# Neighbourhood attention scores: two heads on the two halves of the partitions, three 64-row products each

## The chip, the core and the metric

One NeuronCore of a Trainium2 chip runs the whole program: two layers of a transformer-like trunk on 512 latent and 256 context tokens of 1024 features. The metric is the device time of one execution in microseconds (us), lower is better. The engines are TensorE (PE, its weight loads PEld), VectorE (DVE), ScalarE (ACT), GpSimd (POOL) and SyncE (SP, which issues most DMAs). Each engine works through its own queue in order; a semaphore makes it wait for another one.

## The reference, cut to what matters

The neighbourhood attention has 4 heads of 64 features. A latent token attends to 8 x 32 = 256 latent tokens around it, with a bias that also masks, and to the 256 context tokens; a context token attends to the context only.

```python
q, k, v = jnp.split(p, 3, axis=-1)
q, k = _rms(_heads(q, NA_HEADS), g_q), _rms(_heads(k, NA_HEADS), g_k)
...
s_loc = jnp.einsum('bhrjqd,bhrjkd->bhrjqk', qg, kb).astype(F32) * scale + bias[None]
s_ctx = jnp.einsum('bhrjqd,bhcd->bhrjqc', qg, kc).astype(F32) * scale
p = jax.nn.softmax(jnp.concatenate([s_loc, s_ctx], axis=-1), axis=-1).astype(v.dtype)
o = (jnp.einsum('bhrjqk,bhrjkd->bhrjqd', p[..., :n_loc], vb)
     + jnp.einsum('bhrjqc,bhcd->bhrjqd', p[..., n_loc:], vc))
```

The kernel computes the products of two float32 operands as three products of their high and low parts (high x high, high x low, low x high), which TensorE takes in its faster 32-bit type (fp32r).

## The kernel before

Features lie on the partitions for most products, 128 at a time. A layer is: modulated norm; input projections (for MLA, Hyena and the neighbourhood heads); the neighbourhood attention woven with a Hyena convolution; MLA's attention; output projection; MLP.

*Making queries and keys* (`na_qk`): for keys, then queries, the projection gives 128 tokens on the partitions and 256 features (4 heads) at a time. The tokens are squared, summed and, for keys, scaled by their 1 / rms. A group of two or three token tiles is then transposed by TensorE (L513), two heads (`hp`) at a time, so that head 2 hp has partitions 0 to 63 and head 2 hp + 1 partitions 64 to 127 of a PSUM tile `t`. The split takes each head for itself. For a query, ScalarE copies the high part to the head's own half of `na.q` (L518), and VectorE subtracts it and writes the low part to the *other* half (L519): a column of `na.q[:, h]` holds high and low parts one under the other, 128 rows. For a key, ScalarE copies the high part to its own half of `na.k` (L523), VectorE writes the low part to `na.kl` (L524), and ScalarE copies the high part once more, to the other half of `na.k` (L525).

*Scores* (`na_scores`, for one head, 128 queries and 256 keys) are two matmuls into the same PSUM columns: one on all 128 rows (L550), which gives high x high and low x high together, and one on the 64 rows of the high part with `na.kl` (L552).

*Attention* (`na_attend`) works in units of 128 queries and two heads: 8 units for latent queries in each layer, and 4 for context queries in the first layer alone. A unit's `scores` fill a PSUM tile `s_` of two banks, one for each head, 256 local and 256 context keys: eight matmuls for a latent unit, four for a context unit. VectorE adds the bias (L575), ScalarE copies the context part (L576), then come the softmax (`softmax_rows`, L447 to L460), the transposes of the weights two units later (`turn`, L587), and the product with the values two units after that (`output`, L606: the two heads on two halves of the array's columns). There are two PSUM tiles of `s_`'s kind at this time.

The program is written as generators that take turns (`weave`), here attention with the Hyena convolution at 1 : 1.4; a scheduler then sets the order on each engine from what depends on what. Tiles are placed in SBUF by pools on a left and a right stack; a tile that comes to lie where another one was waits for that one's users.

Of the kernel before, what the change touches and what calls it, by code (L numbers as in the profile page):

```python
# [16 lines left out]
ALU = mybir.AluOpType  # L17
# [19 lines left out]
def r32(ap):  # L37
    return ap.bitcast(F32)
# [3 lines left out]
def kernel(ctx, tc, A, dbg=None, stop=None):  # L42
# [22 lines left out]
    def psum_banks(mm):  # L65
        """all of PSUM: mm tiles of two banks, the rest tiles of one"""
# [52 lines left out]
    def rsqrt(p, out, ms):  # L119
        """out = ms ** -0.5 for ms > 0"""  # L120
# [7 lines left out]
    def mm3(out, s, m, start, stop):  # L128
        """out += (sh + sl).T @ (mh + ml) but for sl.T @ ml"""
# [44 lines left out]
    def modulation_rows(lv, cr, p):  # L174
        """the same by dot products off the tensor engine, features on the partitions"""
# [34 lines left out]
    def sumsq(acc, xT, k, nt, p):  # L210
        """acc += xT[:, k] ** 2"""
# [7 lines left out]
    def norm_rstd(acc, nt, p):  # L219
        """the tokens' 1 / rms, on every partition; comes last, after a turn for others"""  # L220
# [24 lines left out]
    def norm_h(l, n, xT, hh, hl, nt, p):  # L245
        """modulated activations of normed ones, a tile of features at a time"""
# [10 lines left out]
    def norm_stream(l, s, rb, xT, hh, hl, p):  # L257
        """norm_x and norm_h of a stream"""
# [25 lines left out]
    def gemm(out, w, nk, m, streams, woff=0, wstride=128, fill=iter(())):  # L284
        """out[:, tokens] = W.T @ act: w's and m's high and low parts; outs, ws and streams may be lists, k's then shared"""
# [42 lines left out]
    def sin_layer(p, outs, zs, hyc, j):  # L328
        """sin(freq (z + b)) by way of the remainder of the argument by 2 pi; a layer on each half"""
# [15 lines left out]
    def filter_hidden(p, h2):  # L345
        """the filters' hidden activations, both layers', and a row of ones"""
# [15 lines left out]
    def filter_unit(l, st, o, h2, fc, dec, w3, p):  # L362
        """a filter of a layer, stream and order: generators for the time domain and for the spectrum"""
# [60 lines left out]
    def na_bias(l, p, sc):  # L424
        """relative position biases, [query, column block kind, head, key], NEG_INF outside the window"""
# [17 lines left out]
    def softmax_rows(p, sb, n, nh, tag, scale=None, src=None):  # L443
        """sb[:, h, :n] = softmax of scale * src[:, h, :n] over n, for the heads h"""
# [20 lines left out]
    def token_gemm(pts, grp, n, hh, hl, w, fill=iter(())):  # L465
        """pts[token tile][:, :n] = act[:, token tile].T @ w for the token tiles of the group"""
# [13 lines left out]
    def na_v(l, hh, hl, na, kr, fill=iter(())):  # L480
        """values of the neighbourhood heads and MLA's shared rope key, tokens on the partitions"""
# [72 lines left out]
    def na_attend(l, na, nb, mh, ml, p):  # L554
# [5 lines left out]
        def scores(u):  # L560
# [3 lines left out]
            if j >= 4:  # L564
                for hh in range(2):
                    na_scores(s_[:, hh, 0:256], na, 2 * hp + hh, 128 * j, S, 256)
# [1002 lines left out]
```

## Time and profile before

| | |
|---|---|
| runs | 1871.37, 1879.92, 1880.49 us |
| median | 1879.92 us |
| span of the profiled execution, first to last instruction | 1876.5 us |
| TensorE matmul / weight load busy | 96% / 81% |
| VectorE / ScalarE / GpSimd busy | 66% / 44% / 18% |
| mean granted TensorE clock | 0.975 |

For the profiled execution the span is the time that is known; it lies 3.4 us under the median of the runs. Busy shares are means over stages with different limits. "Busy" on TensorE is from a matmul's start to its modelled end, and these overlap, so that 96% doesn't say that it multiplies all the time: the distance from one start to the next does. In the timeline a row is a run of like instructions with its start, its length, the engine, the line and the tiles (out<-in), and in square brackets the idle time of the engine before it and what ended it.

### The profile page before, as it was taken

The numbers are of one execution on the slowest core, as the hardware profiler recorded it, in microseconds if no ns is written. First come the engines' busy times: TensorE is split into PE (matmuls) and PEld (weight loads), VectorE is DVE, ScalarE is ACT, GpSimd is POOL, SyncE is SP. The second block draws the span as 40 slices with busy tenths as digits, with TensorE's granted clock in tenths as the row PEclk, the third lists the DMA queues.
The fourth block names the chain that finished last, engine by engine and source line by source line (L and its number), as shares of the span: only waits on it lengthen the run. The fifth ranks groups of instructions, "written<-read, shape, count | busy, mean of one in ns | idle before, by whom it ended". The sixth has DMA issues, their size and how long they took to land.

```text
span 1876.5 us, 27190 instructions
## 1 busy us (share of the span) xinstructions
PE 1797.2 (96%) x10722; PEld 1519.0 (81%) x10722; DVE 1232.1 (66%) x2127; ACT 824.1 (44%) x1387; POOL 338.1 (18%) x265
## 2 busy tenths in 40 slices
PE   6999978999998999999999999899999999999999
PEld 2688877766686878888888888788777799999997
DVE  5866775866668865666665447887877665555554
ACT  3334435566644543333334124555566653333331
POOL 1523320300034423323232000530300000000000
PEclk9999987999999899999999999899999999999999
DMA  8124423052143333333333212254040022322322
GB/s 336 59 84 144 149 94 100 23 212 62 54 179 124 135 122 123 124 135 127 121 117 120 68 63 94 86 198 138 25 176 24 23 91 90 98 94 90 101 91 79
DMA packets 73247, 205.08 MB, mean 109 GB/s; under 512 B 12540, under 2 KB 24589, under 8 KB 71840
## 3 DMA queue, kind: packets, MB, share of 16 engines
q1 hardware_dynamic: 71520, 198.10, 30.9%
q0 software_dynamic: 1600, 5.24, 0.7%
q8 instruction: 85, 1.39, 0.3%
q14 instruction: 42, 0.34, 0.1%
HBM read 181.30 MB, written 21.23 MB: 108 GB/s over the span
## 4 chain that ended last, share of the span: by engine, by line
PE 66%; DVE 7%; issue 2%; ACT 2%; DMA 2%; POOL 1%; SPq 0%; DVEq 0%; POOLq 0%; ACTq 0%
PE mm L295 46%; PE b L1040 3%; PE mm L1027 3%; PE mm L1374 2%; PE mm L131 2%; PE mm L132 2%; PE mm L133 2%; PE b L1081 1%; DMA wm<-in_w_modr_dram 1%; DVE wm L193 1%; DVE wl L137 1%; PE mm L987 1%; POOL wmp L189 1%; PE b L150 1%; DVE t L1380 1%
## 5 line engine op out<-in xcount | busy, mean ns | idle before, releaser
L295 PE MATMUL mm<-t,wh 128*128 128x512 f32 (+1 forms) x2496 | 495.0, 319 | 1.9 <-DVE t L1064 1.3
L295 PEld LDWEIGHTS mm<-t,wh 128*128 128x128 f32 x2496 | 373.3, 190 | 38.0 <-issue 2.4
L136 ACT ACTIVATE wh<-wr 128x1024 fp32r<-128x1024 f32 (+2 forms) x176 | 184.6, 1050 | 419.1 <-PE mm L295 399.7
L295 PE MATMUL mm<-t,wl 128*128 128x512 f32 (+1 forms) x1248 | 298.5, 317 | 0.0
L189 POOL TENSOR_TENSOR wmp<-wm,t 128x1024 f32<-128x1024 f32 x64 | 169.5, 2655 | 487.1 <-DMA wm<-in_w_modr_dram 314.2
L137 DVE TENSOR_TENSOR wl<-wr,wh 128x1024 fp32r<-128x1024 f32 (+2 forms) x176 | 224.0, 1273 | 35.3 <-ACT wh L136 31.9
L295 PE MATMUL mm<-ah,wh 128*128 128x512 f32 (+1 forms) x768 | 232.8, 357 | 3.9 <-DVE t L1064 3.2
L295 PE MATMUL mm<-al,wh 128*128 128x512 f32 (+1 forms) x768 | 231.9, 356 | 0.0
L295 PE MATMUL mm<-ah,wl 128*128 128x512 f32 (+1 forms) x768 | 231.3, 356 | 0.0
L1064 DVE SCALAR_TENSOR_TENSOR t<-mm,mods,t 128x512 f32<-128x512 f32 x216 | 135.9, 657 | 134.3 <-PE mm L295 127.6
L295 PEld LDWEIGHTS mm<-t,wl 128*128 128x128 f32 x1248 | 194.7, 190 | 16.9
L193 DVE SCALAR_TENSOR_TENSOR wm<-wm,t 128x1024 f32<-128x1024 f32 x64 | 91.1, 1426 | 104.6 <-POOL wmp L189 104.6
L295 PEld LDWEIGHTS mm<-ah,wh 128*128 128x128 f32 x768 | 127.0, 189 | 27.4 <-DVE t L1064 3.5
L295 PEld LDWEIGHTS mm<-al,wh 128*128 128x128 f32 x768 | 127.6, 189 | 20.6
L295 PEld LDWEIGHTS mm<-ah,wl 128*128 128x128 f32 x768 | 126.6, 189 | 21.6
L194 ACT ACTIVATE wmp<-wmp 128x1024 f32<-128x1024 f32 x64 | 67.9, 1060 | 147.3 <-POOL wmp L189 147.3
L137 DVE TENSOR_TENSOR al<-relu,ah 128x768 fp32r<-128x768 f32 (+1 forms) x64 | 68.0, 1064 | 37.2 <-ACT ah L136 37.1
L447 DVE TENSOR_REDUCE mmx<-mm 128x1 f32<-128x768 f32 (+1 forms) x80 | 67.7, 847 | 32.1 <-PE mm L133 31.5
L452 ACT ACTIVATE msb<-mm,mmx,qrs 128x768 f32<-128x768 f32 (+1 forms) x80 | 72.2, 903 | 23.3 <-DVE mmx L449 19.4
L1374 PE MATMUL mm<-t,wh 128*128 128x512 f32 x320 | 76.8, 354 | 2.8 <-DVE t L1064 2.8
L1028 ACT ACTIVATE mpt<-mm 128x768 f32<-128x768 f32 (+1 forms) x80 | 57.6, 725 | 49.4 <-PE mm L1027 49.3
L136 ACT ACTIVATE ah<-relu 128x768 fp32r<-128x768 f32 (+1 forms) x64 | 47.3, 739 | 63.9 <-DVE relu L1127 63.7
(316 smaller groups left out, 3070.2 us busy)
## 6 DMA issues: line engine op xcount, KB each, us to landing
wr<-in_w_ff_dram SPq DMA_DIRECT2D x128, 512.0 KB, 3.6
wm<-in_w_modr_dram SPq DMA_DIRECT2D x64, 512.0 KB, 4.5
wm<-in_w_mod_dram SPq DMA_DIRECT2D x32, 512.0 KB, 7.7
wr<-in_w_in_t_dram SPq DMA_DIRECT2D x18, 512.0 KB, 3.3
qk<-qk_spill SPq DMA_DIRECT2D x9, 576.0 KB, 5.9
qk_spill<-upk SPq DMA_DIRECT2D x12, 384.0 KB, 3.0
kx<-kk POOLq DMA_DIRECT2D x16, 256.0 KB, 2.5
wr<-in_w_in_qk_dram SPq DMA_DIRECT2D x8, 512.0 KB, 4.0
```

What stands on the lines that cost most here:

```text
L136: act.activation(hi, src, AF.Copy)
L137: dve.tensor_sub(lo, src, r32(hi))
L189: pool.tensor_tensor(P[i - MD], W[i - MD], cr[:, 1], ALU.mult)
L193: dve.scalar_tensor_tensor(w, w, 1.0, cr[:, 0], ALU.mult, ALU.mult, accum_out=mods[:, l, v, k, 0:1])
L194: act.activation(pr, pr, AF.Copy, accum_out=mods[:, l, v, k, 1:2])
L295: pe.matmul(out_[:, po:po + b - a], wk[wx], mk[mx][:, a:b], start=(k == 0 and i == 0), stop=(k == nk - 1 and i == 2))
L447: dve.tensor_reduce(mx, src, AX.X, ALU.max, negate=True)
L452: act.activation(sb[:, h, :n], src[:, h, :n], AF.Exp, bias=mx[:, h:h + 1], scale=1.0 if scale is None else scale[:, h:h + 1], accum_out=sm ...
L1027: pe.transpose(tt[:, c * 128:(c + 1) * 128], sb[:, 0, c * 128:(c + 1) * 128], ident)
L1028: act.activation(pt[:, 0:nkt, qt * 128:(qt + 1) * 128], tt[:, :nkt * 128].rearrange("p (c q) -> p c q", q=128), AF.Copy)
L1064: dve.scalar_tensor_tensor(xT[:, m, a:b], t[:, a:b], mods[:, l, v, m, s:s + 1], xT[:, m, a:b], ALU.mult, ALU.add)
L1374: pe.matmul(t[:, a:b], ws[wx], half[mx][:, k % 4, a:b], start=(k == ks[0] and i == 0), stop=(k == 7 and i == 2))
```

## The change

Queries and keys each get a tile for the high and one for the low parts, `qh`, `ql`, `kh`, `kl`, of two heads on 128 partitions each, head 2 hp on the lower and head 2 hp + 1 on the upper half. A split is then one copy and one subtraction on 128 partitions, where a query took two of each on 64 partitions and a key four copies and two subtractions. `na_scores` takes both heads: three products for each on its own 64 rows, the heads by turns. A latent unit's scores are 12 matmuls instead of 8, those of a context unit 6 instead of 4, and a unit's matmuls are written before the first instruction that reads them. On a partition the four tiles take 6 KB less than the three did, so the tiles that are placed after them on the right stack move.

```diff
-                for z in range(2):
-                    h, mine, other = 2 * hp + z, slice(64 * z, 64 * z + 64), slice(64 - 64 * z, 128 - 64 * z)
-                    if which == "q":
-                        hi = na.q[mine, h, to]
-                        act.activation(hi, t[mine], AF.Copy, scale=g[mine])
-                        dve.scalar_tensor_tensor(na.q[other, h, to], t[mine], g[mine], r32(hi),
-                                                 ALU.mult, ALU.subtract)
-                    else:
-                        hi = na.k[mine, h, to]
-                        act.activation(hi, t[mine], AF.Copy)
-                        dve.tensor_sub(na.kl[mine, hp, to], t[mine], r32(hi))
-                        act.activation(na.k[other, h, to], t[mine], AF.Copy)
+                if which == "q":
+                    hi = na.qh[:, hp, to]
+                    act.activation(hi, t, AF.Copy, scale=g)
+                    dve.scalar_tensor_tensor(na.ql[:, hp, to], t, g, r32(hi), ALU.mult, ALU.subtract)
+                else:
+                    split(na.kh[:, hp, to], na.kl[:, hp, to], t)
...
-    def na_scores(out, na, h, q0, k0, n):
+    def na_scores(out, na, hp, q0, k0, n):
+
         q, k = slice(q0, q0 + 128), slice(k0, k0 + n)
-        pe.matmul(out, na.q[:, h, q], na.k[:, h, k], start=True, stop=False)
-        hi = slice(64, 128) if h % 2 else slice(0, 64)
-        pe.matmul(out, na.q[hi, h, q], na.kl[hi, h // 2, k], start=False, stop=True)
+        for i, (qq, kk) in enumerate(((na.qh, na.kh), (na.qh, na.kl), (na.ql, na.kh))):
+            for z in range(2):
+                mine = slice(64 * z, 64 * z + 64)
+                pe.matmul(out[:, z], qq[mine, hp, q], kk[mine, hp, k], start=(i == 0), stop=(i == 2))
...
             if j >= 4:
-                for hh in range(2):
-                    na_scores(s_[:, hh, 0:256], na, 2 * hp + hh, 128 * j, S, 256)
+                na_scores(s_[:, :, 0:256], na, hp, 128 * j, S, 256)
...
+            na_scores(s_[:, :, 0:256], na, hp, 128 * j, a, 256)
+            na_scores(s_[:, :, 256:512], na, hp, 128 * j, S, 256)
             for hh in range(2):
                 h = 2 * hp + hh
-                na_scores(s_[:, hh, 0:256], na, h, 128 * j, a, 256)
-                na_scores(s_[:, hh, 256:512], na, h, 128 * j, S, 256)
...
-        na.q, na.k, na.kl = np_([128, 4, nt], F32R), np_([128, 4, NT], F32R), np_([128, 2, NT], F32R)
+        na.qh, na.ql = np_([128, 2, nt], F32R), np_([128, 2, nt], F32R)
+        na.kh, na.kl = np_([128, 2, NT], F32R), np_([128, 2, NT], F32R)
```

On TensorE, where the attention of the first layer begins, the order before is this. `mm_2725` and `mm_2761` are the score tiles of units 0 and 1, `t_1283` the queries, `t_1284` and `t_1285` the keys' tiles `na.k` and `na.kl`, and `b_2784` a transpose of the Hyena convolution:

```order
L550 MATMUL mm_2761<-t_1284,t_1283 128x256
L552 MATMUL mm_2761<-t_1285,t_1283 128x256
L750 MATMUL b_2784<-ident,t_1289 128x128 x4
L550 MATMUL mm_2725<-t_1284,t_1283 128x256
L552 MATMUL mm_2725<-t_1285,t_1283 128x256
L550 MATMUL mm_2725<-t_1284,t_1283 128x256
L552 MATMUL mm_2725<-t_1285,t_1283 128x256
L550 MATMUL mm_2761<-t_1284,t_1283 128x256
```

The same place of the changed kernel, with `mm_2742` for unit 1 and `mm_2776` for unit 2, `t_1283` for `qh`, `t_1284` for `ql`, `t_1285` for `kh`, `t_1286` for `kl`:

```order
L548 MATMUL mm_2742<-t_1285,t_1283 128x256 x2
L548 MATMUL mm_2742<-t_1286,t_1283 128x256 x2
L548 MATMUL mm_2742<-t_1285,t_1284 128x256 x2
L745 MATMUL b_2769<-ident,t_1290 128x128 x4
L548 MATMUL mm_2776<-t_1285,t_1283 128x256 x2
L548 MATMUL mm_2776<-t_1286,t_1283 128x256 x2
L548 MATMUL mm_2776<-t_1285,t_1284 128x256 x2
```

Before, the second heads of units 0 and 1 stand behind the convolution's transposes, after the first heads of both; now both heads of both units stand ahead of those transposes, and unit 2 follows.

On VectorE, the queue ahead of the first score instruction of the first layer (L575, and L570 in the changed kernel) is this before; L519 are the query splits, L124 to L126 the steps of the queries' 1 / rms:

```order
L126 SCALAR_TENSOR_TENSOR t_91<-rs_t_2670,t_91 128x12
L519 SCALAR_TENSOR_TENSOR t_1283<-b_2681,t_2092,t_1283 64x384
L124 TENSOR_TENSOR rs_t_2670<-t_91 128x12
L519 SCALAR_TENSOR_TENSOR t_1283<-b_2689,t_2092,t_1283 64x384
L125 SCALAR_TENSOR_TENSOR rs_t_2670<-rs_t_2670,nms_2668 128x12
```

And in the changed kernel:

```order
L517 SCALAR_TENSOR_TENSOR t_1284<-b_2668,t_2093,t_1283 128x384
L124 TENSOR_TENSOR rs_t_2651<-t_91 128x12
L137 TENSOR_TENSOR t_2688<-t_1290,t_2687 128x256
L125 SCALAR_TENSOR_TENSOR rs_t_2651<-rs_t_2651,nms_2649 128x12
L137 TENSOR_TENSOR wl_5016<-wr_5014,wh_5015 128x1024
L126 SCALAR_TENSOR_TENSOR t_91<-rs_t_2651,t_91 128x12
L124 TENSOR_TENSOR rs_t_2651<-t_91 128x12
```

Two of the four query splits between the sums of squares and the first score instruction are gone, those between the later steps of the 1 / rms.

## Rows read from the trace of the kernel before

**Rows 1.** The page, its first line.
```profile
span 1876.5 us, 27190 instructions
```
**Rows 2.** Stretches, first layer: length, busy PE, PEld, DVE, ACT, POOL, PEclk, DMA, GB/s.
```profile
303.00:312.00 9.00, 8.28 (x18) 4.65 (x19) 4.26 (x7) 5.25 (x12) 0.00 (x0) 0.50 1.01 345
312.00:320.00 8.00, 8.00 (x31) 6.72 (x30) 2.75 (x5) 6.30 (x18) 0.00 (x0) 0.52 0.09 31
320.00:345.00 25.00, 24.88 (x150) 18.83 (x148) 22.51 (x38) 14.31 (x34) 9.60 (x8) 1.00 0.12 43
345.00:360.00 15.00, 15.00 (x94) 11.61 (x95) 9.91 (x19) 9.61 (x22) 2.83 (x2) 1.00 0.01 2
```
**Rows 3.** Timeline of PE where the query projection ends and scores begin.
```profile
293.58 0.28 PE L131 MATMUL b<-wh,t 128*128 128x256 f32 x1
293.70 0.28 PE L132 MATMUL b<-wl,t 128*128 128x256 f32 x1
...
295.06 0.38 PE L552 MATMUL mm<-t,t 64*128 64x256 f32 x1
295.38 0.38 PE L550 MATMUL mm<-t,t 128*128 128x256 f32 x1
```
**Rows 4.** Timeline of PE, the second heads of the first units.
```profile
302.77 0.58 PE L550 MATMUL mm<-t,t 128*128 128x256 f32 x1 [4.30 <-ACT nsb L576]
303.29 0.58 PE L552 MATMUL mm<-t,t 64*128 64x256 f32 x1
```
**Rows 5.** Timeline of DVE at the same place.
```profile
299.99 0.62 DVE L519 SCALAR_TENSOR_TENSOR t<-b,t,t 64x384 fp32r<-64x384 f32 x1
...
301.67 0.88 DVE L575 SCALAR_TENSOR_TENSOR nsb<-mm,t,t 128x256 f32<-128x256 f32 x2
304.99 0.48 DVE L575 SCALAR_TENSOR_TENSOR nsb<-mm,t,t 128x256 f32<-128x256 f32 x1 [2.45 <-PE mm L552]
307.03 0.48 DVE L575 SCALAR_TENSOR_TENSOR nsb<-mm,t,t 128x256 f32<-128x256 f32 x1 [1.55 <-PE mm L552]
```
**Rows 6.** Stretches, second layer, columns as in rows 2.
```profile
1304.00:1320.00 16.00, 15.64 (x67) 11.43 (x67) 14.92 (x35) 10.93 (x23) 4.74 (x4) 0.99 0.13 37
1320.00:1343.00 23.00, 22.75 (x118) 16.61 (x117) 16.54 (x32) 12.51 (x30) 4.28 (x4) 0.86 0.13 46
1343.00:1360.00 17.00, 15.76 (x98) 12.26 (x96) 14.98 (x24) 8.57 (x20) 9.35 (x8) 1.00 0.00 1
```
**Rows 7.** The chain that ended last, second layer: start, length, engine, tile, line.
```profile
1300.29 0.48 ACT t L525
1300.78 0.49 ACT t L523
...
1303.28 0.88 DVE t L519 x2
```
**Rows 8.** Timeline of PE, output of a unit and transposes of another.
```profile
325.21 1.09 PE L606 MATMUL b<-npt,t 128*64 128x128 f32 x16
326.24 1.09 PE L587 MATMUL b<-ident,nsb 128*128 128x128 f32 x8
```
**Rows 9.** Timelines of DVE and of PE, first layer, making of keys.
```profile
273.87 0.56 DVE L524 TENSOR_TENSOR t<-b,t 64x384 fp32r<-64x384 f32 x1
...
280.48 1.19 PE L801 MATMUL b<-t,zc 128*128 128x128 f32 x4 [4.25 <-DVE zc L780]
```
**Rows 10.** Groups by line from 320 to 375 us: busy, mean ns, idle before.
```profile
L550 PE MATMUL mm<-t,t 128*128 128x256 f32 x26 | 10.5, 406 | 0.1
L552 PE MATMUL mm<-t,t 64*128 64x256 f32 x26 | 9.9, 381 | 0.0
```
**Rows 11.** Groups by line from 1319 to 1343 us.
```profile
L550 PE MATMUL mm<-t,t 128*128 128x256 f32 x13 | 6.0, 462 | 0.0
L552 PE MATMUL mm<-t,t 64*128 64x256 f32 x12 | 5.1, 424 | 0.0
```
**Rows 12.** The chain, second layer, sums of squares: one column a matmul.
```profile
1211.30 3.20 PE b L678 x28
```

## Prediction

> **What bounds the kernel now.** The whole span is 1876.5 us [rows 1], and the change touches two short places of it, one in each layer: the making of the neighbourhood queries and keys, and the attention on them. So the page's shares decide little, and I read the table of stretches for the first layer's attention next [rows 2]. From 303 to 320 us TensorE works all the time, but at a granted clock of 0.50 and 0.52, and VectorE has over half of the time free (4.26 of 9 us, 2.75 of 8 us). From 320 to 345 both are nearly full (24.88 and 22.51 of 25 us); from 345 to 360 TensorE is full and VectorE has 5 us free.
>
> The timeline of TensorE says why it is full. A matmul of 256 columns in a plain stream starts 0.12 us after the one ahead of it; the score matmuls, which go by turns on 128 and on 64 array rows, start 0.32 us apart [rows 3]. At half clock the step is 0.52 us [rows 4]. So about 0.20 us of each score matmul (0.32 - 0.12) is the turn from one row count to the other: the next weights are not loaded under the matmul ahead. There is also a stall of 4.30 us before the second heads of the first two units, which waits for ScalarE's copy of the first heads [rows 4]. VectorE's queue shows both ends of it: its first score instruction, at 301.67, stands behind the query splits of 0.62 us each, and its next two then wait 2.45 and 1.55 us for L552 [rows 5].
>
> In the second layer the order of the bounds is another one [rows 6]: VectorE is full from 1304 to 1320 (14.92 of 16 us), TensorE from 1320 to 1343 (22.75 of 23 us, VectorE 16.54), VectorE again to 1360. The chain of work that ended last runs, just ahead of that, over the key splits' copies on ScalarE and the query splits on VectorE [rows 7].
>
> **The change part by part.** *Scores.* A call for two heads and 256 keys had four matmuls, each at a turn of the row count: 4 x 0.32 = 1.28 us. It has six now, all on 64 rows, the heads alternately on the lower and the upper half. No row of the trace has two matmuls on two row halves, so I bound a pair of them. Below: 0.12 us, one matmul's step [rows 3], if the halves stream at the same time. Above: 0.64 us, if each change of half costs what a change of row count costs (2 x 0.32). Between: 0.24 us, if one follows the other without a gap. The nearest row is the attention output, which has pairs on two column halves of the array: 16 matmuls of 128 columns take 1.09 us, as long as 8 transposes of 128 columns on the whole array [rows 8], so two halves do run at the same time there. I take 0.12 us. Each unbroken run of score matmuls then pays one turn in and one out, 2 x 0.20 = 0.40 us; the order of the changed kernel has 25 such runs (14 in the first layer, 11 in the second). In all, 216 matmuls in 108 pairs: 108 x 0.12 + 25 x 0.40 = 23 us, against 144 x 0.32 = 46 us and some more for those at half clock. That is 23 us off TensorE and more than can reach the end, so the stages count.
>
> *Splits.* A copy or subtraction on 128 partitions replaces two on 64; its time follows the elements of a partition, which stay (384 or 256), so one of each two goes, and of the keys' ScalarE copies three of four.
>
> *First layer, making of keys.* TensorE waits 4.25 us for a product of VectorE, whose rows show no idle time from the key split at 273.87 on to that product; this split of 0.56 us goes [rows 9]. **-0.6 us.**
>
> *First layer, to 303 us.* In the gapless queue ahead of 301.67 two query splits of four go: 2 x 0.62 [rows 5]. **-1.25 us.**
>
> *First layer, 303 to 320.* By the new order all scores of units 0 and 1 stand ahead of the first VectorE read of them. At 12 x 0.12 + 0.80 = 2.2 us they are done long before it, and VectorE's waits of 2.45 and 1.55 us go. The 20 score matmuls at half clock (20 x 0.52 = 10.4 us) become those of units 2 and 3, 12 pairs at twice 0.12 us and two turns, 3.7 us. Late next is ScalarE, busy 11.55 us of these 17 [rows 2], one table load among it. So of 17 us at most 5.5 can go; I take the two waits and one more. **-5 us.** No gain from an earlier return of the clock is in it.
>
> *First layer, from 320 us.* 52 score matmuls [rows 10] x 0.32 = 16.6 us become 72 (the units ahead have taken more), 36 x 0.12 + 11 x 0.40 = 8.7 us: 7.9 us off TensorE. VectorE, late next, has 7.6 us free from 320 to 360 (2.49 + 5.09) [rows 2], and not all at the right places. **-4.5 us**, between 0 and -7.6.
>
> *Second layer, to 1320.* VectorE is the bound. Four query splits of 0.44 us or a little more go, 1.9 us; ahead of them copies L525 and L523 of 0.49 us and their waits go from ScalarE's queue, which held the last query tile up: 1.3 us [rows 7]. **-3.2 us.** The scores' own gain there is hidden by VectorE.
>
> *Second layer, 1320 to 1343.* 25 score matmuls [rows 11], four of them at half clock, are 4 x 0.52 + 21 x 0.32 = 8.8 us; three units after are 18 pairs and four runs, 2.2 + 1.6 = 3.8 us: 5.0 us off a full TensorE, with VectorE free for 6.5 us [rows 6]. **-4 us.** After 1343 VectorE is the bound again and I count **-0.5 us.**
>
> *Memory.* The tiles shrink by 6 KB on a partition, so later tiles lie elsewhere and some loads wait for other work (the load of the second layer's first transform matrix takes over a wait from that of the second). These sit on SP's queue well ahead of their use; I price them at zero, up to 2 us if one falls due.
>
> Sum: 0.6 + 1.25 + 5 + 4.5 + 3.2 + 4 + 0.5 = 19 us. The profiled span lies 3.4 us under the median of the runs; I take the 19 us off the median, as what lies around the span is not changed: 1879.9 - 19 = 1861.
>
> **The rivals.** *Loads one after the other.* Each matmul brings its own load of 128 columns. Where the matmul is next to nothing (L678, one column), 28 of them take 3.20 us, 0.114 us each [rows 12]: that is the rate of loads. If two halves' loads don't run at the same time, a pair takes 0.23 us and not 0.12. Then the part from 320 us is 36 x 0.23 + 4.4 = 12.7 us, 3.9 us off and perhaps 2.3 gained; 1320 to 1343 is 4.1 + 1.6, 3.1 off and 2.5 gained; 303 to 320 gives 4. Sum 14 us: **1866**. For it: no row shows two loads of 128 columns at once. Against it: the column pairs [rows 8]. The Trainium skill has a rule on each side here. "TensorE: Matmul & The Clock Gate", section on LDWEIGHTS, says that a load costs by its columns, not its rows, 107 ns by its formula, so that a load for half of the rows saves nothing; by it alone a pair would take an estimated 0.21 us, and the row of L678 agrees. "TensorEngine Tiling (Array Packing)", Key Properties, says that tiles load and multiply in parallel; by it a pair would take 0.12 us, and no run shows that yet for rows.
>
> *Each change of half drains the array.* The mechanism is that of the rows now: 0.20 us at each turn, also from one half to the other. A pair takes 0.64 us, so a unit 12 x 0.32 = 3.84 us and not 8 x 0.32 = 2.56. It decides from 0.36 us a pair on: three pairs and half a run's 0.40 us are then 1.28 us, as before. From 320 us this adds 72 x 0.32 - 16.6 = 6.4 us to a full TensorE, from 1320 to 1343 36 x 0.32 - 8.8 = 2.7, and the units at half clock some 4; the scores of units 0 and 1 (24 x 0.32 = 7.7 us) take the first 1.25 us back, and 1304 to 1320 adds 36 x 0.32 - 24 x 0.32 = 3.8, less the 3.2 there. Sum about +13 us: **1893**. For it: the row count's turn does drain. Against it: the halves are the same shape, and column halves show no drain [rows 8].
>
> *VectorE and ScalarE take the gain.* Pairs run as forecast, but the waits only move: in the places where TensorE is full, VectorE's queue is so near full that nothing comes through. Then 4.5 and 4 us fall to 1 each and the 5 us to 3: about 9.5 us, **1870**. For it: 22.51 of 25 us [rows 2]. Against it: in 345 to 360 and 1320 to 1343 VectorE does have room.
>
> **How the numbers follow.** Pairs at 0.12 us with the stages as summed: 0.55, 1861. Loads one after the other: 0.22, 1866. Gain taken by VectorE: 0.15, 1870. Drain at each half: 0.08, 1893. The range leaves out the last; its low end takes all of TensorE's 23 us and the splits' 5 us with some of the clock (-30 us), its high end a gain of 7 us. About 0.5% (9.4 us) is what a measurement of this kernel can tell from no change: below 1870.5 lie nearly all of the first two cases and half of the third, 0.79; slower than 1889 is the drain, 0.06; 0.15 between.
>
> **What would show it.** In the profile of after: the score matmuls' starts in pairs a few ns apart with steps of 0.12 us from pair to pair (0.23: loads; 0.32 from one to the next: drain); two waits for the scores fewer on VectorE near 304 us; the transposes of unit 0 about 6 us earlier against the last key matmul; VectorE with under 4 us free in the 40 us after the first full-clock unit; as many key and query splits as before halved, each with the old duration. I am wrong if the scores' steps come out as forecast and the end of either attention moves by less than half of its sum.

## The result, and the profile after

The changed kernel takes 1862.13 us (median of four runs, 1856.33 to 1863.73), the kernel before 1878.87 us beside it (1871.37 to 1880.49): a ratio of 0.9924 with a 95% interval of 0.9895 to 0.9952, so 9 to 20 us less. 1861 was forecast. The profiled execution spans 1860.1 us, 16.4 less than that of [rows 1]. The head of its page, engine by engine (busy us, share of the span, instructions):

```profile
span 1860.1 us, 27267 instructions
PE 1770.8 (95%) x10794; PEld 1504.4 (81%) x10794; DVE 1227.3 (66%) x2111; ACT 807.1 (43%) x1355; POOL 339.4 (18%) x265
```

TensorE's timeline in the first layer's attention of the changed kernel (start, duration, line, operation, shape, count, idle time before and what ended it) answers to [rows 3, 4]:

```profile
294.41 0.98 PE L548 MATMUL mm<-t,t 64*128 64x256 f32 x12
296.00 0.98 PE L548 MATMUL mm<-t,t 64*128 64x256 f32 x12
301.38 2.27 PE L548 MATMUL mm<-t,t 64*128 64x256 f32 x24 [3.72 <-ACT nsb L571]
305.41 1.94 PE L582 MATMUL b<-ident,nsb 128*128 128x128 f32 x8 [1.77 <-DVE nsb L460]
310.87 3.72 PE L757 MATMUL b<-ux,t 128*128 128x256 f32 x16
```

A unit's scores are twelve matmuls (L548) in 0.98 us, six steps of 0.12 us and the tail of the last; before they were eight at 0.32. The scores of units 2 and 3 still wait for ScalarE (3.72 us). They are 24 matmuls in 2.27 us, the second half of them at half clock, where 20 had 0.52 us each. The transposes of unit 0 (L582) start at 305.41 and not at 311.73, the first products of the long convolution (L757) at 310.87 and not at 319.02. These two places in the kernel before:

```profile
311.73 1.72 PE L587 MATMUL b<-ident,nsb 128*128 128x128 f32 x7 [0.72 <-DVE nsb L460]
319.02 1.37 PE L762 MATMUL b<-ux,t 128*128 128x256 f32 x4
```

VectorE's timeline at the same place (columns as above) answers to [rows 5]:

```profile
299.25 0.87 DVE L570 SCALAR_TENSOR_TENSOR nsb<-mm,t,t 128x256 f32<-128x256 f32 x2
300.33 0.87 DVE L570 SCALAR_TENSOR_TENSOR nsb<-mm,t,t 128x256 f32<-128x256 f32 x2 [0.21 <-ACT nsb L571]
301.35 2.35 DVE L447 TENSOR_REDUCE nmx<-nsb 128x2 f32<-128x1024 f32 x2
...
307.45 0.48 DVE L570 SCALAR_TENSOR_TENSOR nsb<-mm,t,t 128x256 f32<-128x256 f32 x1 [2.18 <-ACT npt L584]
```

The first score read starts at 299.25 and not at 301.67, four reads follow each other without a wait for TensorE, and what VectorE waits for next is ScalarE. By stretches (us, busy time and count of PE, PEld, DVE, ACT, POOL, granted clock, DMA share, GB/s), against [rows 2]:

```profile
301.00:309.00 8.00, 5.86 (x41) 5.35 (x42) 4.93 (x10) 7.33 (x16) 0.00 (x0) 0.58 1.03 326
309.00:334.00 25.00, 21.34 (x157) 16.87 (x157) 22.21 (x34) 15.36 (x39) 9.60 (x8) 0.98 0.23 83
334.00:350.00 16.00, 16.00 (x113) 13.24 (x112) 10.81 (x22) 11.53 (x28) 2.46 (x2) 0.93 0.01 3
350.00:376.00 26.00, 21.70 (x177) 17.15 (x176) 19.09 (x42) 13.54 (x41) 6.77 (x7) 1.00 0.24 85
```

TensorE is no longer full in three of the four stretches. From 301 to 309 ScalarE is (7.33 of 8 us), from 309 to 334 VectorE nearly (22.21 of 25). The half clock, which held from 303 to 320 before (0.50 and 0.52), is over by 309. In the second layer, against [rows 6], columns as above:

```profile
1290.00:1304.00 14.00, 13.02 (x86) 10.35 (x85) 12.37 (x29) 10.07 (x22) 4.80 (x4) 1.00 0.34 98
1304.00:1326.00 22.00, 18.68 (x134) 14.73 (x135) 18.95 (x35) 14.01 (x34) 4.80 (x4) 0.92 0.14 49
1326.00:1343.00 17.00, 14.24 (x100) 11.59 (x98) 15.83 (x24) 7.65 (x19) 9.49 (x8) 0.91 0.00 0
```

There too TensorE has 3 us free in each of the last two stretches, where it had been full for 23.

**The affected stages by themselves.** In every kernel of this study two kinds of instruction frame the stage that changes: the first key transposes (L513) and the first transposes of the attention that follows (L987 before, L982 after). Before, then after:

```profile
256.78 1.06 PE L513 MATMUL b<-ident,tok 128*128 128x128 f32 x3 [4.54 <-DVE tok L507]
383.41 2.17 PE L987 MATMUL mm<-ident,qk 128*96 128x128 f32 x18
1284.61 0.30 PE L513 MATMUL b<-ident,tokk 128*128 128x128 f32 x1 [0.19 <-DVE tokk L507]
1374.78 1.73 PE L987 MATMUL mm<-ident,qk 128*96 128x128 f32 x14
```

```profile
256.36 1.06 PE L513 MATMUL b<-ident,tok 128*128 128x128 f32 x3 [4.18 <-DVE tok L507]
374.80 2.17 PE L982 MATMUL mm<-ident,qk 128*96 128x128 f32 x18
1273.80 0.30 PE L513 MATMUL b<-ident,tokk 128*128 128x128 f32 x1 [0.19 <-DVE tokk L507]
1357.21 1.73 PE L982 MATMUL mm<-ident,qk 128*96 128x128 f32 x14
```

So the stage is 126.63 us long before and 118.44 after in the first layer, 90.17 and 83.41 in the second: 8.2 + 6.8 = 15.0 us. The other 1.4 us of the span's 16.4 are elsewhere, in parts that the change doesn't touch. The same two differences are taken from the trace of every kernel below. They agree with the medians to within 3 us, though the medians also carry what the clock does in the rest of the program. A stage's length is that of one execution, and whole executions of the kernel before range from 1867.8 to 1889.6 us, so that a microsecond or two between two kernels of this table shows little by itself. Each median stands against that of the kernel before beside it, 1877.37 us for E1 to E4, 1877.07 for E5 to E8 and 1879.44 for E9 to E11:

| kernel | first layer | second | both, against before | median, against before |
|---|---|---|---|---|
| before | 126.63 | 90.17 | | |
| changed | 118.44 | 83.41 | -15.0 | -16.7 |
| E1, heads one after the other | 118.50 | 83.31 | -15.0 | -14.2 |
| E2, splits by head | 121.64 | 86.77 | -8.4 | -9.8 |
| E3, before, reads behind | 124.17 | 89.05 | -3.6 | -3.0 |
| E4, before, by row count | 119.15 | 87.21 | -10.4 | -10.2 |
| E5, scaling on ScalarE | 121.08 | 84.30 | -11.4 | -8.7 |
| E6, before, scaling on ScalarE | 132.43 | 91.32 | +7.0 | +7.5 |
| E7, six then six | 120.41 | 85.95 | -10.4 | -10.5 |
| E8, one half | 121.85 | 91.41 | -3.5 | -5.1 |
| E9, no first scaling | 116.71 | 85.97 | -14.1 | -15.4 |
| E10, early scaling on VectorE | 117.85 | 83.67 | -15.3 | -15.5 |
| E11, convolution earlier | 121.19 | 86.61 | -9.0 | -11.9 |

### The profile page after: what moved, and what is told of

It reads as the page before. It is cut to its first block, busy times and chain, and to the rows that moved or that the text cites. A ratio compares the mean times of both kernels' runs of the same rounds, so it can differ in the third digit from the quotient of the medians.

```text
span 1860.1 us, 27267 instructions
## 1 busy us (share of the span) xinstructions
PE 1770.8 (95%) x10794; PEld 1504.4 (81%) x10794; DVE 1227.3 (66%) x2111; ACT 807.1 (43%) x1355; POOL 339.4 (18%) x265
## 5 line engine op out<-in xcount | busy, mean ns | idle before, releaser
L137 DVE TENSOR_TENSOR wl<-wr,wh 128x1024 fp32r<-128x1024 f32 (+2 forms) x176 | 228.0, 1296 | 37.3 <-ACT wh L136 33.8
L295 PEld LDWEIGHTS mm<-al,wh 128*128 128x128 f32 x768 | 126.4, 188 | 20.2
L137 DVE TENSOR_TENSOR al<-relu,ah 128x768 fp32r<-128x768 f32 (+1 forms) x64 | 68.2, 1066 | 37.1 <-ACT ah L136 37.1
L447 DVE TENSOR_REDUCE mmx<-mm 128x1 f32<-128x768 f32 (+1 forms) x80 | 67.7, 847 | 32.1 <-PE mm L133 31.5
```

What stands on the lines that cost most here:

```text
L137: dve.tensor_sub(lo, src, r32(hi))
L295: pe.matmul(out_[:, po:po + b - a], wk[wx], mk[mx][:, a:b], start=(k == 0 and i == 0), stop=(k == nk - 1 and i == 2))
L447: dve.tensor_reduce(mx, src, AX.X, ALU.max, negate=True)
```

## The experiments

**E1: is the alternation of the heads worth anything?**

```
-        for i, (qq, kk) in enumerate(((na.qh, na.kh), (na.qh, na.kl), (na.ql, na.kh))):
-            for z in range(2):
+        for z in range(2):
+            for i, (qq, kk) in enumerate(((na.qh, na.kh), (na.qh, na.kl), (na.ql, na.kh))):
```

> The changed kernel with one edit: a call's three products of the first head come first, then the three of the second, so that two neighbours share a half of the rows but at one place. Theory (two halves work at once, and that is what the alternation is for): the score matmuls start 0.12 us apart one by one and not two by two, a call of six takes 0.72 us and not 0.36, so 36 x 0.36 = 13 us more on TensorE in all, of which the stages bound by TensorE pass on some: three units, six calls, 2.2 us in the second layer from 1320 us of the kernel before, and 2 to 4 us in the first layer; 4 to 6 us slower than the changed kernel, 1866 to 1868. Rival (the gain came from the turns of the row count and the waits alone, the pairs are worth nothing at the end): within 2 us of the changed kernel, 1862, with steps of 0.12 us all the same.

1863.2 us, a ratio of 0.9911 (0.9882 to 0.994): as the changed kernel. But for a third reason. A unit's run on TensorE, and what follows it:

```profile
321.33 0.98 PE L548 MATMUL mm<-t,t 64*128 64x256 f32 x12
322.24 0.99 PE L601 MATMUL b<-npt,t 128*64 128x128 f32 x14
```

Twelve matmuls still take 0.98 us, as in the changed kernel, so they are in pairs, although three of one head stand ahead of three of the other. That order is also the one in TensorE's queue: the scheduler leaves it as the program has it. Strictly in order it would be nine steps, 0.36 us more: only the third of one head could run with the first of the other. (Two on the same half start 0.12 us apart, see E8.) So a matmul for the free half of the rows starts ahead of two that are queued for the busy half. The edit didn't take the pairs away, and the experiment says nothing on their price.

**E7: how far does that reach?** The changed kernel, a unit's six products of the first head, then the six of the second:

```
+            for z in range(2):
+                na_scores(s_[:, :, 0:256], na, hp, 128 * j, a, 256, (z,))
+                na_scores(s_[:, :, 256:512], na, hp, 128 * j, S, 256, (z,))
```

> The changed kernel, but a unit's six products of the first head come first, both calls of it, and then the six of the second. In the run with three of a head in a row the matmuls started two by two all the same, one of each head. Theory (each half of the rows takes its own instructions ahead of those queued for the other half, as far as a look-ahead reaches): with six in a row either still 12 in 6 steps of 0.12 us, 0.98 us for a unit, if the look-ahead is six or more, or some of them one by one, up to 12 steps, 1.4 to 1.7 us. Rival (the pairs came from the order in the program after all): 12 steps of 0.12 us, 1.7 us for a unit.

```profile
316.73 1.32 PE L548 MATMUL mm<-t,t 64*128 64x256 f32 x12
317.98 1.09 PE L602 MATMUL b<-npt,t 128*64 128x128 f32 x16
```

1.32 us: nine steps, three of them pairs, where TensorE's queue has six of one head and then six of the other. In order it would be eleven. The first pair is the third step, so TensorE looks ahead over a few matmuls and not over five. It is a single run (1866.58 us). Its stages are 10.4 us shorter than before, those of the changed kernel 15.0; 1.7 us of the difference are a stretch of half clock on the convolution's products of L796 (L797 in E7: 28 matmuls in 8.00 us for 6.31). What this order costs at the end is not settled.

**E8: the price of the pairs.** Both heads' products on the lower half, where the first head's queries and keys are; the second head's scores are left out:

```
-                mine = slice(64 * z, 64 * z + 64)
+                mine = slice(0, 64)
```

> The changed kernel, but both heads' products use the lower half of the array's rows, with the first head's queries and keys twice (the second head's scores are left out), so that no two score matmuls can run at once: the price of the pairs. Theory by the sum of the forecast: 12 steps of 0.12 us and not 6 in a unit, 36 x 0.36 = 13 us more on TensorE, 4 to 6 us at the end, 1866 to 1868. Rival (TensorE has room for it in both attentions, as VectorE bounds them; the gain came from fewer turns and from the waits): within 2 us of the changed kernel, 1861 to 1864.

```profile
322.52 1.69 PE L548 MATMUL mm<-t,t 64*128 64x256 f32 x12
324.14 1.09 PE L601 MATMUL b<-npt,t 128*64 128x128 f32 x16
```

Twelve steps of 0.12 us, 0.71 more for a unit, and 1872.0 us: a ratio of 0.9976 (0.9959 to 0.9993), 10 us slower than the changed kernel. My 4 to 6 was too little, the rival's 2 more so. By stages 3.4 us are lost in the first layer and 8.0 in the second. The second layer's windows of this kernel (columns as above) show what is in the 8.0:

```profile
1319.00:1331.00 12.00, 12.00 (x48) 8.88 (x47) 7.91 (x15) 5.57 (x13) 1.22 (x2) 0.57 0.24 87
1331.00:1350.00 19.00, 17.58 (x130) 14.97 (x126) 14.75 (x26) 10.66 (x25) 4.82 (x4) 1.00 0.00 1
1350.00:1362.00 12.00, 11.34 (x47) 9.27 (x48) 8.70 (x14) 4.06 (x10) 4.79 (x4) 0.57 0.01 1
```

At 0.57 some 10 of each 12 us ran at half clock, 20 us in all. In the changed kernel, at 0.92 of 22 us and 0.91 of 17, it was 7. At half clock the steps are 0.21 us and not 0.12, so 14 more such us account for up to 7 of the 8.0. In the first layer 28 matmuls of L796 take 8.00 us for 6.31 in the changed kernel, 1.7 of the 3.4. By this estimate the pairs by themselves are worth some 3 us at the end, and some 10 with what the clock adds. All twelve runs (1868.62 to 1878.9) lie above all of the changed kernel (to 1863.73); why the clock falls more often with single matmuls is not shown.

**E3: the order alone.** The kernel before with all scores of a unit ahead of the first read:

```
             for hh in range(2):
+                na_scores(s_[:, hh, 0:256], na, 2 * hp + hh, 128 * j, a, 256)
+                na_scores(s_[:, hh, 256:512], na, 2 * hp + hh, 128 * j, S, 256)
+            for hh in range(2):
                 h = 2 * hp + hh
-                na_scores(s_[:, hh, 0:256], na, h, 128 * j, a, 256)
-                na_scores(s_[:, hh, 256:512], na, h, 128 * j, S, 256)
```

> The kernel before with one edit: the eight score matmuls of a unit (both heads) are written ahead of the first read of them; products, splits and turns of the row count stay. Theory (a third part of the gain is the order alone): TensorE's wait of 4.30 us for ScalarE's copy of the first heads goes, VectorE's waits of 2.45 and 1.55 us shrink to what 8 matmuls at 0.32 us leave; the transposes of unit 0 come some 4 us earlier: 1875. Rival (the order is worth nothing without cheaper products, as TensorE is full there at half clock): 1879, the transposes of unit 0 within 1 us of where they were.

1874.41 us, a ratio of 0.999 (0.9962 to 1.0017). The total is the theory's, the mechanism the rival's: the transposes of unit 0 start 55.6 us after the first key transposes (55.0 before). The stretch, and TensorE's rows at its end:

```profile
301.00:309.00 8.00, 7.92 (x16) 4.56 (x16) 3.39 (x5) 5.71 (x13) 0.00 (x0) 0.50 1.00 346
```

```profile
308.74 0.58 PE L552 MATMUL mm<-t,t 64*128 64x256 f32 x1
309.25 1.97 PE L588 MATMUL b<-ident,nsb 128*128 128x128 f32 x8
```

The order does what it was to do for units 0 and 1: VectorE reads their scores without a wait for TensorE, and TensorE's wait of 4.30 us for ScalarE is 2.83. But VectorE then waits for unit 2 (1.86 us for L552) and has nothing to do (3.39 of 8 us busy), as sixteen matmuls of units 2 and 3 at half clock, 0.51 us each, stand ahead of the transposes. The order brings the transposes forward only with cheap scores behind it. Its 3 us cannot be told from none.

**E4: the turns of the row count.** The kernel before, its own products and splits, with two turns a unit (`first` are the products on 128 rows):

```
+            for first in ((True, False), (False, True))[c]:
+                for z in range(2):
+                    if first:
+                        pe.matmul(out, na.q[:, h, q], na.k[:, h, k], start=(c == 0), stop=(c == 1))
+                    else:
+                        pe.matmul(out, na.q[hi, h, q], na.kl[hi, hp, k], start=(c == 1), stop=(c == 0))
```

> The kernel before with its own products and splits, but a unit's eight score matmuls ahead of the reads and in the order of the row count: two on 128 rows, four on 64 rows with the heads by turns, two on 128 rows, so two turns of the row count a unit and not eight. Theory (turns cost 0.20 us each, and two 64-row matmuls on different halves run at once): 4 x 0.12 + 2 x 0.12 + 0.40 = 1.12 us a unit, as much as in the changed kernel (6 pairs and two turns); so the time is that of the changed kernel plus the splits, 1867, and the same as that of the changed kernel with splits by head. Rival (the pairs themselves, not the turns, carry the gain): near the kernel before with the reads behind, 1875.

1867.22 us, a ratio of 0.9941 (0.9919 to 0.9964): the theory's number. A unit in its TensorE timeline:

```profile
295.31 0.48 PE L556 MATMUL mm<-t,t 128*128 128x256 f32 x2
295.73 0.50 PE L558 MATMUL mm<-t,t 64*128 64x256 f32 x4
296.16 0.51 PE L556 MATMUL mm<-t,t 128*128 128x256 f32 x2
296.50 0.65 PE L754 MATMUL b<-ident,t 128*128 128x128 f32 x4
```

From 295.31 to 296.50 it is 1.19 us for what had taken 2.56 with a turn at each matmul. Two turns of 0.20 us and six steps of 0.12 make 1.12. The four 64-row matmuls between are two pairs. Against E3 (which differs from it only by the turns and pairs) this is 7 us by the medians.

**E2: the splits.** The changed kernel's scores with queries and keys split by head, and the two further key copies into a tile that nothing reads:

```
-                    act.activation(hi, t, AF.Copy, scale=g)
-                    dve.scalar_tensor_tensor(na.ql[:, hp, to], t, g, r32(hi), ALU.mult, ALU.subtract)
+                    for mine in (slice(0, 64), slice(64, 128)):
+                        act.activation(na.qh[mine, hp, to], t[mine], AF.Copy, scale=g[mine])
+                        dve.scalar_tensor_tensor(na.ql[mine, hp, to], t[mine], g[mine], ...)
...
-                    split(na.kh[:, hp, to], na.kl[:, hp, to], t)
+                    for mine, other in (...):
+                        split(na.kh[mine, hp, to], na.kl[mine, hp, to], t[mine])
+                        act.activation(na.kd[other, hp, to], t[mine], AF.Copy)
```

> The changed kernel's scores, but queries and keys split head by head on 64 partitions, as before, with the two extra copies of each key tile on ScalarE into a tile that nothing reads. Theory (the splits' part of the forecast): the first layer's keys 0.6 us later, its first score read 1.25 us later, the second layer's 3.2 us: 5 us slower than the changed kernel, 1867. Rival (they hide in slack): 1862, the first score read of each layer where it is in the changed kernel.

1867.6 us, a ratio of 0.9932 (0.9908 to 0.9956), 5.5 more than the changed kernel: the theory's number. The two intervals overlap, so the traces have to show the cause, and they do: against the first key transposes the first score read comes 2.1 us later than in the changed kernel in the first layer and 4.7 in the second. By stages it is 3.2 and 3.4 us; 1.7 of the 3.2 are a stretch of half clock on the convolution's 28 matmuls (L800 here, 7.98 us for 6.31), and not the splits. E4 and E2 come to the same time, as the theory had it: one has the old products without most of their turns, the other the new ones, both the old splits.

**E5, E6, E9: does VectorE keep back the rest?** The changed kernel gains only 0.5 us of the 4.5 forecast from 320 us on (next section). E5 moves the first heads' scaling from VectorE to ScalarE, E6 does so in the kernel before, E9 leaves it out of the changed kernel. E5 and E6:

```
-            if h % 2:
+            if h % 2 or tag == "n":
                 act.activation(sb[:, h, :n], sb[:, h, :n], AF.Copy, scale=rc[:, h:h + 1])
```

and E9:

```
-            else:
+            elif tag != "n":
                 dve.tensor_scalar(sb[:, h, :n], sb[:, h, :n], rc[:, h:h + 1], None, ALU.mult)
```

> The changed kernel with one step moved: the first head's scaling by 1 / sum in the neighbourhood softmax (L460, 0.49 us, 1.49 us where GpSimd works at the same time) goes from VectorE to ScalarE (0.72 us each, as the second head's). In the first layer that takes 6 x 0.49 + 2 x 1.49 + 4 x 0.35 = 7.3 us off VectorE and puts some 8 us on ScalarE. Theory (VectorE, full from 309 us of the changed kernel on, keeps back what the scores save on TensorE): the end of the first layer's attention comes 3 to 5 us earlier against its start than in the changed kernel; in all 1857 to 1860. Rival (VectorE is not what holds that part, but the chain over ScalarE): no earlier or up to 3 us later, 1862 to 1865.

> The same move in the kernel before (L460 to ScalarE). Theory: there TensorE is full from 320 to 345 us (24.88 of 25 us) beside VectorE (22.51), so less comes through than in the changed kernel: the end of the first layer's attention within 1.5 us of where it was against its start, in all 1877 to 1880. Rival (VectorE or ScalarE hold both kernels alike): the same shift as in the changed kernel, in either direction.

> The changed kernel without the first head's scaling by 1 / sum on VectorE (L460 of the neighbourhood softmax, 20 of them; the first heads' weights stay unscaled), and nothing in its place: 7.3 us less for VectorE in the first layer, 5 to 7 us in the second, no work added to ScalarE. It asks what set the end of the first attention where the scores' saving didn't come through. Theory A (VectorE, gapless from 314 to 334 us of the changed kernel): the end of that attention comes 3 to 5 us earlier against its start, in all 1854 to 1858. Theory B (the chain of the long convolution over VectorE's and GpSimd's products, which slow each other: 0.83 or 1.22 us for the same product of VectorE): VectorE's time goes into its own longer products and waits, the end comes less than 1.5 us earlier, in all 1859 to 1862.

E5 took 1868.33 us (0.9946, 0.9929 to 0.9963) and E6 1884.6 us (1.003, 1.0011 to 1.0049). Both lose, 6 and 7.5 us, so the move says nothing for VectorE. That ScalarE's longer scaling (0.72 us for 0.49) costs more than VectorE's free time brings is the likely reason, and not shown; in E5 1.7 us of the loss are a stretch of half clock on L796 (28 matmuls in 8.00 us). E6's first stage is 5.8 us longer than before and E5's 2.6 longer than the changed kernel's, which is neither E6's theory (within 1.5) nor its rival (the same shift). E9 took 1864.07 us (0.9919, 0.9895 to 0.9944), no less than the changed kernel. Its trace is between the theories. The changed kernel's first scores, the second eight products of the convolution's L785 and its last but one stage (L796), then the same of E9:

```profile
294.41 0.98 PE L548 MATMUL mm<-t,t 64*128 64x256 f32 x12
...
331.91 2.81 PE L785 MATMUL b<-zx,t 128*128 128x256 f32 x8 [0.27 <-DVE zx L775]
...
362.15 6.31 PE L796 MATMUL b<-t,zx 128*128 128x256 f32 x28 [2.88 <-DVE zx L775]
```

```profile
292.99 0.98 PE L548 MATMUL mm<-t,t 64*128 64x256 f32 x12
...
328.26 1.99 PE L785 MATMUL b<-zx,t 128*128 128x256 f32 x8 [1.95 <-DVE zx L775]
...
357.07 8.00 PE L796 MATMUL b<-t,zx 128*128 128x256 f32 x28 [2.88 <-DVE zx L775]
```

From the scores to L796 it is 67.7 us in the changed kernel and 64.1 in E9: 3.7 earlier, of 7.3 us that VectorE has less to do. Then L796's 28 matmuls take 8.00 us for 6.31, as a stretch of half clock falls on them, and 1.7 of the 3.7 are gone. The second layer's stage is 2.6 us longer than in the changed kernel. But the 3.7 us are not all VectorE's. The changed kernel is at half clock from 333 to 336 us (granted 0.50), in the L785 shown (2.81 us), and until 309; E9 is at full clock from 303 to 357 us (granted 0.99 and 1.00), with 1.99 us for the same eight products. So VectorE's load is at most half of the answer: the stage ends 1.7 us earlier where theory A has 3 to 5, and the total is theory B's.

**E10: ScalarE at the start.** In the first three units of the first layer the second head's scaling goes to VectorE:

```
-        softmax_rows(p, sb, 512, 2, "n")
+        softmax_rows(p, sb, 512, 2, "n", dv=(l == 0 and u < 3))
```

> The changed kernel with the second head's scaling of the first three units of the first layer on VectorE (0.49 us) and no longer on ScalarE (0.72 us each): the move that failed, the other way round and only where ScalarE is full (15.59 of 17 us from 303 to 320). Theory (ScalarE sets the pace from 301 to 312 us): the transposes of units 1 and 2 and the first products of the convolution come 1 to 2 us earlier, in all 1860 to 1861. Rival (VectorE's wait for ScalarE's sums comes back elsewhere): no change, 1862.

```profile
292.04 0.97 PE L548 MATMUL mm<-t,t 64*128 64x256 f32 x12
...
303.03 1.06 PE L582 MATMUL b<-ident,nsb 128*128 128x128 f32 x8 [1.10 <-DVE nsb L460]
...
312.20 3.69 PE L757 MATMUL b<-ux,t 128*128 128x256 f32 x16
...
356.99 8.00 PE L796 MATMUL b<-t,zx 128*128 128x256 f32 x28 [2.88 <-DVE zx L775]
```

The second sixteen of the convolution (L757) start 20.2 us after the first scores, against 22.7 in the changed kernel (at 317.13): 2.6 us earlier, where I expected 1 to 2, and L796 2.8 earlier. Most of this is the clock and not ScalarE: the transposes of unit 0 start 11.0 us after the first scores in both kernels, and the sixteen that follow from there (L582, then L745) take 1.9 us for 3.5, as E10 is at full clock from 303 us on (granted 1.00 to 320) and the changed kernel from 309. That is 1.7 of the 2.6, so it is not shown that ScalarE sets the pace. Again L796 takes 8.00 us, and the stage ends 0.6 us shorter. 1863.98 us, a ratio of 0.9917 (0.9893 to 0.9942): no gain that can be told.

**E11: the convolution earlier.**

```
-        weave((na_attend(l, na, nb, mh, ml, sc), 1.0), (conv, (1.4, 1.4)[l]))
+        weave((na_attend(l, na, nb, mh, ml, sc), 1.0), (conv, (2.0, 1.4)[l]))
```

> The changed kernel with more of the long convolution's turns per turn of the first layer's attention (2.0 and not 1.4), so that its VectorE and GpSimd products start earlier, into the 5.6 us that VectorE has free from 303 to 320 us, and TensorE's waits there are filled. Theory (the convolution's chain is what ends last in the first attention, and the scores' saving can only come through if it starts earlier): first products of GpSimd 2 to 4 us earlier, end of the attention 2 to 4 us earlier, in all 1858 to 1860. Rival (ScalarE, full there, has to make the convolution's copies as well, and the softmax is held up in its place): no gain or up to 4 us slower, 1862 to 1866.

1867.57 us, a ratio of 0.9932 (0.9911 to 0.9953): the rival, at its slow end or past it. GpSimd's first product came 2.0 us earlier against the first scores, and the stage ended 2.8 us later, 1.7 of them by half clock on L796 (24 matmuls in 7.13 us, 5.45 in E4). None of these versions can be told from the changed kernel as faster.

## Why the prediction was right, term by term

The time and the likeliest case came out as forecast: **pairs at 0.12 us**. The two matmuls of a pair mostly start 2 to 5 ns apart, at most 11, and the pairs 0.119 us apart; a run pays 0.20 us on its way in and 0.14 to 0.20 on its way out. The case of loads one after the other (0.23 us a pair) and that of a drain at each half (0.32 a matmul) are out by the 0.98 us of a unit. The Trainium skill has the rule for this, "TensorEngine Tiling (Array Packing)", Key Properties, that tiles load and multiply in parallel, and the trace now agrees for row halves with loads of 128 columns: 0.12 us a pair, and 0.12 us for a single one in E8. What "TensorE: Matmul & The Clock Gate", section on LDWEIGHTS, says of a load's cost by columns agrees too: in the trace of the kernel before a load for 64 rows (L552) takes 183 ns and one for 128 rows (L550) 187, by the medians. It didn't make the pair dearer.

- *First layer, to 303 us (-0.6 and -1.25).* Right as a sum: the first score read comes 2.0 us earlier against the first key transposes (42.9 us behind them and not 44.9), and E2 gives 2.1 back. The part that I placed in the making of keys is not seen apart: the first scores start 38.0 us after the first key transposes in both kernels.
- *303 to 320 (-5).* Against the first key transposes the transposes of unit 0 come 5.9 us earlier, as forecast, and the first products of the convolution (L757 at 310.87; L762 at 319.02 before) 7.7 earlier. With the terms ahead I had forecast 6.9 by then. The rest can be the earlier end of the half clock, which I had left out of the sum: a granted 0.58 in the 8 us from 301, and 0.98 after, for a half clock of 17 us before; no run separates it. E3 shows that the order, on which I built the two waits, takes them away and by itself brings nothing at the transposes; the cheap scores of units 2 and 3 are the condition.
- *First layer from 320 us (-4.5).* The mis-sized term: 7.7 us were gained by then and 8.2 at the stage's end, so it gave **0.5**. TensorE did save its time (52 score matmuls 0.32 us apart became 36 pairs 0.12 us apart), and then waited. Its waits in the changed kernel from there on:

```profile
325.66 2.09 PE L785 MATMUL b<-zx,t 128*128 128x256 f32 x8 [1.64 <-issue]
331.32 0.33 PE L582 MATMUL b<-ident,nsb 128*128 128x128 f32 x1 [1.76 <-DVE t L137]
355.97 1.10 PE L796 MATMUL b<-t,zx 128*128 128x256 f32 x4 [0.88 <-DVE us0x L766]
362.15 6.31 PE L796 MATMUL b<-t,zx 128*128 128x256 f32 x28 [2.88 <-DVE zx L775]
```

  These four are 7.2 us; before, the one wait of this kind was 1.3 us, the last row below. They come in the convolution's chain, whose products on VectorE and GpSimd follow each other, and in a split on VectorE (L137); for the first of them the profile names no releaser. That VectorE has 7.6 us free in 40 was the wrong question to the right rows: it has them at the end, and where the chain runs, in the changed kernel, none:

```profile
320.00:330.00 10.00, 7.92 (x76) 5.85 (x74) 9.99 (x16) 4.10 (x10) 5.57 (x5) 1.00 0.00 1
```

```profile
371.85 6.31 PE L801 MATMUL b<-t,zx 128*128 128x256 f32 x28 [1.26 <-DVE zx L780]
```

  My rival "VectorE and ScalarE take the gain" is what happened in this stage (its terms add up to 10 us and not to the 9.5 that I gave it), and by E9 VectorE's load is at most half of it. A half-clock stretch around 333 us, with none there before, is a further part. One sign that I had named failed with this term: VectorE was to have under 4 us free in the 40 us after the first full-clock unit, and it has 5.3 (34.66 us busy from 320 to 360).
- *Second layer.* -7.7 was forecast, the stage is 6.8 shorter. The transposes of unit 0 come 4.3 us earlier against the first key transposes (forecast 3.2 to 1320), the rest of the stage gives 2.4 (forecast 4.5): TensorE's saving shows as idle time there too.
- *Splits in all.* 5.05 forecast, 5.5 by the medians and 6.6 by the stages of E2, or 4.9 without the half clock on its L800.
- *Memory moves.* Nothing that can be seen, as forecast.

So of the sum of 19 us the stages gave 15.0: two terms were about 1 us too small, and two were 2 and 4 too large. Another 1.4 us came from the rest of the program, where I had forecast nothing. That the median came within 1.2 us of the forecast is partly luck: beside it the kernel before took 1878.87 us, and 16.7 us is what the change gained.

What stays open: what holds the first layer's late gain beside VectorE's load, and why a stretch of half clock falls on L796 (or the same products under another number) in E2 and in E5 to E11 and not in the changed kernel, E1, E3 and E4.

## What to carry to other kernels

If short matmuls alternate between row counts, count the turns before anything else: at 0.20 us each they cost more here than the products of 0.12 us, and ordering the same products by row count (E4) brought 10 of the 15 us of stage that the new layout brought. Products of 64 rows belong on both halves at once, close to each other in the queue, and then the operands can be split on all 128 partitions in one instruction. And a saving on the engine that is full is worth only what the next chain lets through: read its free time in the stretch where that chain runs, not over the whole stage.

## What was not expected of the hardware

- TensorE starts matmuls out of the order of its queue when they are for different halves of the rows, and so it is not true of it, as said at the start, that each engine works through its queue in order: E1's twelve go in six steps, E7's in nine. The Trainium skill, "TensorE: Matmul & The Clock Gate", Part 3, The mechanism, says that matmuls start and end strictly in order; the run lengths of these two traces (0.98 and 1.32 us, with 0.98 for the alternated order and 1.69 for twelve single steps) differ from that, and the measurement decides here.
- The clock can return a gain or take it. Before, TensorE waited for 4.30 us up to 302.77 and was at half clock until 320 (granted 0.53 from 299 to 303, 0.50 and 0.52 after), at work nearly all the time from 303 on; the changed kernel waits for 3.72 us at this place, and the clock is back by 309 (1.00 from 309 to 320). The cheap scores are not all of the reason: in E3, with the dear ones, it is back by 313 (1.00 from 313 to 320). In E2 and in E5 to E11 a stretch at half clock took some 1.7 us back from the first layer's stage, in E8 up to 7 from the second's.
- VectorE's scaling of 128 x 512 takes 0.49 us, or up to 1.49 us where GpSimd multiplies at the same time (L460 in the changed kernel).
